# The opening of a fused attention block on one core: loads, casts and squares rearranged, a gate's tanh and a rotary product moved

## The chip, the cores and the metric

The kernel runs on one core of one Trainium2 chip. A core has a tensor engine (PE, which multiplies matrices and also transposes), a vector engine (DVE), a scalar engine (ACT), GpSimd (POOL), and a queue (SP) from which this kernel starts its DMAs. The engines run side by side, each working its own instructions in order, and wait for each other through semaphores. Matrix products land in PSUM, which DVE and ACT read; the other memory on the core is SBUF. The metric is the device time of one execution in microseconds. Three executions of the kernel before took 598.47, 598.74 and 599.65 us; the median, 598.74, is the time to beat.

## The reference

One decoder block for 512 tokens (16 learned meta tokens in front), width 1024, float32: a normalised input, one joint projection, two attention branches (a latent-attention branch with rotary positions, and one with a forget gate), gates, and an output projection.

```
u = rmsnorm(h, pre_norm_g)                      # h: 528 x 1024
proj = u @ w_in                                 # 1024 x 7600
(cq, ckv, k_pe_raw, z_mla, fq, fk, fv, f_logit, z_fox, gate_a, gate_b) = split(proj)
q  = rmsnorm(cq)  @ w_uq ;  kv = rmsnorm(ckv) @ w_ukv
k_pe = rope(k_pe_raw, pos)
o_mla = attention(q, k, v, scale)               # 16 heads, causal
o_fox = attention(fq, fk, fv, scale, cumulative log forget gate)
y_mla = (o_mla * silu(z_mla)) @ w_br_mla ;  y_fox = (o_fox * silu(z_fox)) @ w_br_fox
mixed = (sigmoid(gate_a) * y_mla + sigmoid(gate_b) * y_fox) @ w_out
out = (h + rmsnorm(mixed))[16:]
```

## The kernel before

Tokens are worked in tiles: tiles 0 to 3 hold 128 real tokens each, tile 4 the 16 meta tokens. A float32 product is made of three products of rounded parts: every operand `x` is split into a high part (`xh`, a cast) and a low part (`xl`, the difference), and `mm` is called for high x high, low x high and high x low. That is why each weight is cast (`wsh`, `wh`) and then subtracted (`wsl`, `wl`), and why every transposed activation is written twice, `uTh` by ACT and `uTl` by DVE.

The opening does, for every tile `t`: load it (`load_h`, tile `ht`); sum its squares and take the reciprocal root (`squares`, which leaves the result in `st`); scale it into `hn` (`scaled`); transpose it on PE in two halves of four blocks of 128 columns, each half in one PSUM bank (`turn`, tile `pt`); write `uTh` and `uTl` from the bank, block by block (`turned`; the tile of meta tokens in `turned_all`); and multiply with the small weights, the 432 columns of `w_in` for `cq`, `ckv`, `k_pe_raw` and the forget gate (`small`, result `psm`, accumulated over eight blocks `k`). `back` then normalises and rotates `psm` into `sm`, and `latent` transposes that (`pc`). The small weights come in four loads of two blocks each (`wsr`, two DMAs per load), are cast by `small_hi` and subtracted by `small_lo`. The vector `gcol` holds the gain of the first norm, transposed on PE from `g8` (the product `gps`).

At the start PE multiplies a zero tile (`spun`), and it does so again where it would wait. For PE, the program order is the written order (a manual schedule). On the other engines a scheduler orders the instructions by priority, except for those handed to `pin`, which stay in the order in which they are written. `issue_after` places an instruction behind a given one of its engine.

After the opening, the products of queries, keys, values and gates (`fq`, `fk`, `v`, `z`, `pg`) are interleaved with the attention of eight pairs of heads, two branches each. An attention stage computes scores (`st`), exponentials (`sf`), and in `norm` the normalised weights `pn`, a high part by ACT and a low part by DVE; then a transposing DMA and the product with the values. `z_unit` makes a gate: the product `z`, a tanh on ACT into `sil`, and a product on DVE that reads the accumulator again. Accumulators come from a pool of three PSUM buffers (`acc`), which the next products take in turn as they come free.

Of the kernel before, what the change touches and what calls it, by code (L numbers as in the profile page):

```python
# [22 lines left out]
D = 1024  # L23
# [31 lines left out]
def block_kernel(ctx: ExitStack, tc: tile.TileContext, x, meta_tokens, pre_norm_g, w_in, fox_forget_b,  # L55
# [201 lines left out]
    with ExitStack() as ph:  # L257
# [28 lines left out]
        load_h(1)  # L286
# [10 lines left out]
        def small_hi(c, copy):  # L297
            return copy(wsh[:, 2 * c : 2 * c + 2, :], wsr[c])

        def small_lo(c, eng):  # L300
            cs = slice(2 * c, 2 * c + 2)
            return eng.tensor_tensor(out=wsl[:, cs, :], in0=wsr[c], in1=f32(wsh[:, cs, :]), op=ALU.subtract)
# [19 lines left out]
        def squares(t, pin):  # L322
# [5 lines left out]
            if t == 0:  # L328

                for i, sl in enumerate(halves):  # L330
                    pin(nc.scalar.activation(hn[:, sl], ht[:, sl], AF.Square, accum_out=st1[:, 2 + i : 3 + i]))
                pin(nc.vector.tensor_scalar(out=st1[:, 0:1], in0=st1[:, 2:3], scalar1=1.0 / D, scalar2=EPS, op0=ALU.mult,
                                            op1=ALU.add))
                pin(nc.scalar.activation(st1[:, 1:2], st1[:, 3:4], AF.Sqrt, bias=st1[:, 0:1], scale=1.0 / D))
# [5 lines left out]
        def scaled(t, pin):  # L340
            rows = 128 if t < 4 else META
            for sl in halves if t == 0 else [slice(0, D)]:
# [39 lines left out]
        def small(t, which, ks=range(KD)):  # L382

            d0, q0 = (META + 128 * t, 0) if t < 4 else (0, R_Q)
            if t not in psms:
                psms[t] = acc("psm4")[:, 0:NSM] if t == 4 else pps.tile([128, NSM], F32, tag="psm", name=f"psm{t}")
            ts = slice(d0, d0 + 128)
            for k in ks:
                for q, (u, w) in enumerate(((uTh, wsh), (uTl, wsh), (uTh, wsl))):
                    if q in which:  # L390
                        mm(psms[t][:, q0:], u[:, k, ts], w[:, k, q0:], start=(k == 0 and q == 0),
                           stop=(k == KD - 1 and q == 2))

        def back(t):
# [10 lines left out]
            tm = pa.tile([128, 2, 2, 16], F32, tag="tm", name=f"tm{t}")  # L405
            for i in range(2):
                for cs in range(2):
                    nc.vector.tensor_tensor(out=tm[:rows, i, cs], in0=psm[:rows, k0 + 16 * i : k0 + 16 * i + 16],
                                            in1=rt[:rows, t, 2 * i + cs], op=ALU.mult)
            nc.vector.tensor_tensor(out=sm[:rows, k0 : k0 + 32].rearrange("p (a b) -> p a b", a=2), in0=tm[:rows, 0],  # L410
                                    in1=tm[:rows, 1], op=ALU.add)
            rstd(st2[:rows, 2 + both[0][2] : 4], st2[:rows, both[0][2] : 2], 1, 0, rows)
            nc.scalar.copy(sm[:rows, k0 + 32 :], psm[:rows, k0 + 32 :])
# [32 lines left out]
        scaled(0, pin)  # L446
        pin(nc.vector.tensor_copy(gcol, gps[:, 0, 0:KD]))
        turn(0)
        for _ in range(4):
            mm(spun, KP[1][:, 0:128], KP[1][:, 0:512], start=True, stop=True)  # L450
        squares(1, pin)
        scaled(1, pin)
        for c in range(3):
            pin(small_hi(c, nc.gpsimd.tensor_copy))
        turned(0, 0, range(KD), pin)
        small(0, (0,), range(2))
        turn(1)
        turned(0, 1, range(KD), pin)
        pin(small_lo(0, nc.gpsimd))
        turned(1, 0, range(KD), pin)  # L460
        turned(1, 1, range(KD), pin)
        pin(small_hi(3, nc.scalar.copy))
        small(0, (1,), range(2))
        small(0, (0, 1), range(2, 6))
        small(1, (0, 1), range(6))
        small(0, (0, 1), range(6, KD))
        small(1, (0, 1), range(6, KD))
        for c in (1, 2, 3):
            pin(small_lo(c, nc.vector))
# [6 lines left out]
        small(0, (2,))  # L476
# [58 lines left out]
    with ExitStack() as att:  # L535
# [26 lines left out]
        masks = []  # L562
# [163 lines left out]
        def attention(br, pr):  # L726
# [64 lines left out]
            def norm(g):  # L791
                def fn():
# [14 lines left out]
                    for b in GRP[g]:  # L807
                        for h in range(2):
# [5 lines left out]
                            nc.scalar.activation(hi, sf, AF.Copy, scale=rib)  # L814
# [400 lines left out]
```

## Time and profile before

| what | value |
|---|---|
| median of three executions | 598.74 us |
| the profiled execution | 598.62 us |
| its span on the core | 596.5 us |
| PE busy | 588.3 us (99%) |
| DVE busy | 380.2 us (64%) |
| ACT busy | 343.3 us (58%) |
| POOL busy | 201.6 us (34%) |

The span runs from the first to the last instruction in the profile; the profiled execution's own time is 2.1 us longer. All places in time below are microseconds from the start of the span. A row of the profile in order of time reads: start, duration, engine, source line, operation, the tile written and the tiles read, partitions x elements, count; in brackets stands how long the engine had idled before, and who released it. Several rows of one kind that follow each other are merged, and the duration is then that of the whole group. In the chain of waits each step goes back to what released the one after it.

### The profile page before, as it was taken

Reading aid. Unit: us, or ns where it says so; the run is one execution under the profiler, and the core shown is the slowest. Engines: PE = TensorE matmul, PEld = TensorE weight load, DVE = VectorE, ACT = ScalarE, POOL = GpSimd, SP = SyncE. Lnnn points to the kernel's source line nnn. Section 1 sums busy time; section 2 is a strip of 40 time slices with the busy share of each in tenths; the row PEclk is TensorE's granted clock in tenths of the full one; section 3 lists DMA queues with packets and bytes.
Section 4 is the critical chain, followed back from the end, with each engine's and each line's share of the span. In section 5 each row is a group of like instructions: output and inputs, shape, how many; then the busy total and the mean of one; then the engine's idle time right before and its main releaser. Section 6 shows DMA issues by size and latency. Waiting matters only on the chain.

```text
span 596.5 us, 10744 instructions
## 1 busy us (share of the span) xinstructions
PE 588.3 (99%) x3697; PEld 497.3 (83%) x3697; DVE 380.2 (64%) x1096; ACT 343.3 (58%) x785; POOL 201.6 (34%) x271
## 2 busy tenths in 40 slices
PE   8999999999999999999999999999999999999996
PEld 7989779889888888798898898878888888888884
DVE  5944876775776775757758747855634524367857
ACT  7846775784774775757748747842123423353753
POOL 3317646455458463544544544430000000000000
PEclk9999999999999999999999999999999999999999
DMA  8535599999994998896986987978523332333503
GB/s 295 119 78 170 122 173 248 219 175 232 166 218 113 221 220 219 185 188 166 177 197 166 194 162 154 194 166 297 168 77 100 105 105 73 106 106 102 215 2 141
DMA packets 219998, 97.45 MB, mean 163 GB/s; under 512 B 131456, under 2 KB 209672, under 8 KB 219944
## 3 DMA queue, kind: packets, MB, share of 16 engines
q1 hardware_dynamic: 219944, 96.77, 70.1%
q8 instruction: 29, 0.48, 0.3%
q14 instruction: 25, 0.20, 0.1%
HBM read 62.36 MB, written 3.97 MB: 111 GB/s over the span
## 4 chain that ended last, share of the span: by engine, by line
PE 95%; ACT 1%; DVE 1%; DMA 1%; issue 0%; SPq 0%; POOL 0%; DVEq 0%; ACTq 0%; POOLq 0%
PE z L97 16%; PE pg L97 15%; PE py L97 15%; PE v L97 9%; PE st L97 8%; PE fk L97 8%; PE fq L97 8%; PE ov L97 5%; PE x L97 4%; PE psm L97 3%; PE mq L97 2%; PE mk L97 1%; PE ppe L97 1%; PE y L97 1%; DMA wsr<-in_w_in_dram 1%; ACT uTh L367 0%
## 5 line engine op out<-in xcount | busy, mean ns | idle before, releaser
L103 POOL TENSOR_TENSOR wl<-wraw,wh 128x1024 fp32r<-128x1024 f32 (+2 forms) x62 | 119.5, 1935 | 92.8 <-ACT wh L130 70.0
L130 ACT CAST wh<-wraw 128x1024 fp32r<-128x1024 f32 (+1 forms) x80 | 83.1, 1043 | 116.0 <-PE pg L97 38.5
L787 ACT ACTIVATE sf<-sf,nb 128x272 f32<-128x272 f32 (+3 forms) x128 | 72.5, 568 | 16.5 <-DVE nb L779 15.0
L815 DVE SCALAR_TENSOR_TENSOR pn<-sf,ri,pn 128x128 f16<-128x128 f32 (+3 forms) x128 | 68.6, 576 | 6.7 <-ACT pn L814 6.4
L103 DVE TENSOR_TENSOR wl<-wraw,wh 128x1024 fp32r<-128x1024 f32 x34 | 41.6, 1222 | 42.4 <-ACT wh L130 42.4
L814 ACT ACTIVATE pn<-sf,ri 128x128 f16<-128x128 f32 (+3 forms) x128 | 61.3, 550 | 9.3 <-ACT sf L787 7.4
L97 PE MATMUL z<-uTh,wh 128*128 128x512 f32 x128 | 50.9, 398 | 0.0
L97 PE MATMUL pg<-uTh,wh 128*128 128x512 f32 x128 | 50.3, 393 | 0.0
L97 PE MATMUL z<-uTl,wh 128*128 128x512 f32 x128 | 50.1, 392 | 0.0
L97 PE MATMUL z<-uTh,wl 128*128 128x512 f32 x128 | 50.0, 390 | 0.0
L97 PE MATMUL pg<-uTh,wl 128*128 128x512 f32 x128 | 49.8, 389 | 0.0
L97 PE MATMUL pg<-uTl,wh 128*128 128x512 f32 x128 | 49.8, 389 | 0.0
L97 PE MATMUL py<-gh,wh 128*128 128x512 f32 x128 | 49.8, 389 | 0.0
L97 PE MATMUL py<-gl,wh 128*128 128x512 f32 x128 | 49.8, 389 | 0.0
L97 PE MATMUL py<-gh,wl 128*128 128x512 f32 x128 | 49.8, 389 | 0.0
L97 PE MATMUL st<-hlk,hlq 64*128 64x272 f32 (+3 forms) x480 | 45.5, 308 | 0.0
L97 PEld LDWEIGHTS st<-hlk,hlq 64*128 64x128 f32 x480 | 34.6, 185 | 6.0 <-ACT vh L702 2.8
L683 DVE TENSOR_REDUCE vsc<-v 128x1 f32<-128x272 f32 (+1 forms) x32 | 13.2, 433 | 39.9 <-PE v L97 39.9
L97 PE MATMUL v<-uTh,wl 128*128 128x256 f32 (+1 forms) x128 | 36.5, 285 | 0.0
L97 PE MATMUL fk<-uTl,wh 128*128 128x256 f32 (+1 forms) x128 | 36.4, 285 | 0.0
L97 PE MATMUL fk<-uTh,wh 128*128 128x256 f32 (+1 forms) x128 | 36.4, 285 | 0.0
L97 PE MATMUL v<-uTl,wh 128*128 128x256 f32 (+1 forms) x128 | 36.4, 285 | 0.0
(233 smaller groups left out, 1461.5 us busy)
## 6 DMA issues: line engine op xcount, KB each, us to landing
wraw<-in_w_in_dram SPq DMA_DIRECT2D x56, 512.0 KB, 4.5
cbp<-c_dram SPq DMA_DIRECT2D x16, 264.0 KB, 4.7
wraw<-in_w_br_fox_dram SPq DMA_DIRECT2D x8, 512.0 KB, 8.3
tb<-in_w_out_dram SPq DMA_DIRECT2D x8, 512.0 KB, 4.9
wraw<-in_w_br_mla_dram SPq DMA_DIRECT2D x8, 512.0 KB, 3.4
wraw<-in_w_out_dram SPq DMA_DIRECT2D x6, 512.0 KB, 3.7
xr<-in_x_dram SPq DMA_DIRECT2D x4, 512.0 KB
out_dram<-yo SPq DMA_DIRECT2D x8, 256.0 KB, 2.0
```

The lines of the kernel that those rows point to most:

```text
L97: nc.tensor.matmul(*a, **k)
L103: return eng.tensor_tensor(out=lo, in0=src, in1=f32(hi), op=ALU.subtract)
L130: nc.scalar.copy(wh[:, :n], raw[:, :n])
L683: nc.vector.tensor_reduce(out=sc[:, i : i + 1], in_=ps, op=ALU.max, axis=AX.X, apply_absolute_value=True)
L787: exps[g] = nc.scalar.activation(sf, sf, AF.Exp, bias=sums["nb"][:, h, b : b + 1], scale=-1.0, accum_out=sums["su"][:, h, b : b + 1]).ins
L814: nc.scalar.activation(hi, sf, AF.Copy, scale=rib)
L815: nc.vector.scalar_tensor_tensor(out=lo, in0=sf, scalar=rib, in1=hi, op0=ALU.mult, op1=ALU.subtract)
```

## The change

It has these parts:

- SP: the first load of the small weights is issued ahead of tile 1's load instead of behind it.
- Casts and subtractions of the small weights go by single blocks of 128 rows (432 columns) instead of pairs (864): of the casts, four are now on ACT (blocks 1, 3, 5, 7) and four on POOL; of the subtractions, blocks 0 and 1 go singly and 2-3 together to POOL, 4-5 and 6-7 to DVE.
- The squares of tile 1 are made in halves, one on DVE and one on ACT, as are its scalings; between them stand the first copies of tile 0.
- The spins of PE: five, then `gps`, then three; and three after the first `psm` products of tile 0, of which there are now five ahead of tile 1's transposes instead of two.
- `back`: the second pair of rotary products is written to free columns of the PSUM bank of `psm` instead of SBUF.
- The tanh of the first forget-branch gate (pair 0) is put behind the last of the stage's `pn` copies on ACT.

```diff
-        load_h(1)
...
             wsr.append(r)
+            if c == 0:
+                load_h(1)
+
+        def small_hi(k, copy):
+            return copy(wsh[:, k, :], wsr[k // 2][:, k % 2, :])
...
+        def squares(t, pin, first=lambda: None, second=lambda: None):
...
+            if t < 2:
                 for i, sl in enumerate(halves):
+                    sums = st1[:, 2 + i : 3 + i]
+                    if t and i == 0:
+                        pin(nc.vector.tensor_tensor_reduce(out=hn[:, sl], in0=ht[:, sl], in1=ht[:, sl], scale=1.0, scalar=0.0,
+                                                           op0=ALU.mult, op1=ALU.add, accum_out=sums))
+                    else:
+                        pin(nc.scalar.activation(hn[:, sl], ht[:, sl], AF.Square, accum_out=sums))
+                first()
+                plus, root = (3, 2) if t else (2, 3)
+                pin(nc.vector.tensor_scalar(out=st1[:, 0:1], in0=st1[:, plus : plus + 1], scalar1=1.0 / D, scalar2=EPS, op0=ALU.mult,
                                             op1=ALU.add))
+                second()
+                pin(nc.scalar.activation(st1[:, 1:2], st1[:, root : root + 1], AF.Sqrt, bias=st1[:, 0:1], scale=1.0 / D))
...
-            tm = pa.tile([128, 2, 2, 16], F32, tag="tm", name=f"tm{t}")
+            tm = [pa.tile([128, 2, 16], F32, tag="tm", name=f"tm{t}"), psm[:, NSM : NSM + 32].rearrange("p (c f) -> p c f", c=2)]
...
-        for _ in range(10):
-            mm(spun, KP[1][:, 0:128], KP[1][:, 0:512], start=True, stop=True)
+        spin(5)
         gps = ppt.tile([128, 4, 128], F32, tag="pt", name="gps")
         tps(gps[:, 0, 0:KD], g8, ident[0:KD, 0:KD])
+        spin(3)
         squares(0, pin)
+        scaled(0, pin, lambda: pin(nc.vector.tensor_copy(gcol, gps[:, 0, 0:KD])))
         turn(0)
+        pin(small_hi(0, nc.gpsimd.tensor_copy))
+        pin(small_lo(0, 1, nc.gpsimd))
+        turned(0, 0, range(2), pin)
+        pin(small_hi(1, nc.scalar.copy))
+        turned(0, 1, range(2), pin)
+
+        def before_sum():
+            turned(0, 0, range(2, 4), pin)
+            turned(0, 1, [2], pin)
+        squares(1, pin, before_sum, lambda: turned(0, 1, [3], pin))
         scaled(1, pin)
+        turned(0, 0, range(4, 6), pin)
...
+        small(0, (0,), range(2))
+        small(0, (1,), range(2))
+        small(0, (2,), [0])
+        spin(3)
         turn(1)
...
-                with tc.high_priority(offset=60):
+                with tc.high_priority(offset=60), nullcontext() if pr or not br else tc.issue_after(normed[0]):
                     ins = nc.scalar.activation(sil, pz, AF.Tanh, scale=0.5)
```

How the instructions stand now, at three places. In these rows stand the source line, the operation, the tile written and the tiles read, the size, and a count; tile numbers behind a name tell buffers apart. PE at the start of the program, before (`hn_169` is tile 0 scaled, `hn_193` tile 1):

```order
L97 MATMUL spun<-KPL 128x512 x10
L100 MATMUL gps<-ident,g_119 128x8
L100 MATMUL pt_0_179<-ident,hn_169 128x128 x4
L100 MATMUL pt_1_184<-ident,hn_169 128x128 x4
L97 MATMUL spun<-KPL 128x512 x4
L97 MATMUL psm_210<-wsh,uTh 128x432 x2
L100 MATMUL pt_0_213<-ident,hn_193 128x128 x4
L100 MATMUL pt_1_218<-ident,hn_193 128x128 x4
L97 MATMUL psm_210<-wsh,uTl 128x432 x2
```

The same place in the changed program (`hn_167` is tile 0, `hn_194` tile 1):

```order
L97 MATMUL spun<-KPL 128x512 x5
L100 MATMUL gps<-ident,g_119 128x8
L97 MATMUL spun<-KPL 128x512 x3
L100 MATMUL pt_0_177<-ident,hn_167 128x128 x4
L100 MATMUL pt_1_182<-ident,hn_167 128x128 x4
L97 MATMUL psm_217<-wsh,uTh 128x432 x2
L97 MATMUL psm_217<-wsh,uTl 128x432 x2
L97 MATMUL psm_217<-wsl,uTh 128x432
L97 MATMUL spun<-KPL 128x512 x3
L100 MATMUL pt_0_226<-ident,hn_194 128x128 x4
L100 MATMUL pt_1_231<-ident,hn_194 128x128 x4
```

Three more products of tile 0 now stand ahead of tile 1's transposes, and three spins between. ACT between the root for tile 0 and the first copies of tile 1, before; in brackets are the semaphores that a row waits for, named by the engine or the DMA that raises them:

```order
L334 ACTIVATE st_0_170<-st_0_170 128x1 [waits DVE_49,Activation_49]
L337 ACTIVATE hn_193,st_1_194<-ht_122 128x1024 [waits DMAHW3_49]
L317 ACTIVATE st_1_194<-st_1_194,eps_t 128x1 [waits Activation_49]
L367 ACTIVATE uTh<-pt_0_179,gcol 128x128 [waits DVE_49,PE_49]
L367 ACTIVATE uTh<-pt_0_179,gcol 128x128 x3
```

ACT at the same place in the changed program, down to tile 0's fifth copy:

```order
L343 ACTIVATE st_0_168<-st_0_168 128x1 [waits DVE_49,Activation_49]
L378 ACTIVATE uTh<-pt_0_177,gcol 128x128 [waits DVE_49,PE_49]
L378 ACTIVATE uTh<-pt_0_177,gcol 128x128
L299 CAST wsh<-wsr_124 128x432 [waits DMAHW4_49,DMAHW3_49]
L337 ACTIVATE hn_194,st_1_195<-ht_127 128x512 [waits DMAHW5_49]
L378 ACTIVATE uTh<-pt_0_177,gcol 128x128 [waits DVE_49]
L378 ACTIVATE uTh<-pt_0_177,gcol 128x128
L343 ACTIVATE st_1_195<-st_1_195 128x1 [waits DVE_49]
L378 ACTIVATE uTh<-pt_1_182,gcol 128x128 [waits PE_49]
```

Tile 1's Square and root stood ahead of all copies of tile 0; now two copies and a cast stand ahead of its Square, and two copies between the Square and the root. DVE in that stretch of the changed program (the instruction named ISA is the half of the squares, with the read of its sum):

```order
L375 SCALAR_TENSOR_TENSOR uTl<-pt_0_177,gcol,uTh 128x128 [waits DVE_49,PE_49,Activation_49]
L375 SCALAR_TENSOR_TENSOR uTl<-pt_0_177,gcol,uTh 128x128
L334 ISA hn_194,st_1_195<-ht_127 128x512 [waits DMAHW5_49]
L334 ISA st_1_195 128x1
L375 SCALAR_TENSOR_TENSOR uTl<-pt_0_177,gcol,uTh 128x128 [waits Activation_49]
L340 TENSOR_SCALAR st_1_195<-st_1_195 128x1
L375 SCALAR_TENSOR_TENSOR uTl<-pt_0_177,gcol,uTh 128x128
L344 RECIPROCAL st_1_195<-st_1_195 128x1 [waits Activation_49]
L354 TENSOR_SCALAR hn_194<-ht_127,st_1_195 128x512 [waits DVE_49]
```

The small sum that ACT's root needs (L340) stands behind a `uTl` that waits for ACT's copies. ACT in the first attention stage, before:

```order
L814 ACTIVATE pn_715<-sf_873,ri_872 128x2x128 [waits Activation_49] x2
L718 ACTIVATE sil_1043<-z_957 128x512 [waits PE_49]
L814 ACTIVATE pn_715<-sf_873,ri_872 128x3x128 [waits Activation_49]
L814 ACTIVATE pn_715<-sf_873,ri_872 128x3x128
L814 ACTIVATE pn_716<-sf_921,ri_872 128x4x128 [waits DVE_49,Activation_49]
L814 ACTIVATE pn_716<-sf_921,ri_872 128x4x128 [waits Activation_49]
L244 CAST hlq_1055<-mq_1048 128x512 [waits PE_49]
```

And in the changed program:

```order
L845 ACTIVATE pn_720<-sf_878,ri_877 128x2x128 [waits Activation_49] x2
L845 ACTIVATE pn_720<-sf_878,ri_877 128x3x128 [waits Activation_49]
L845 ACTIVATE pn_720<-sf_878,ri_877 128x3x128
L845 ACTIVATE pn_721<-sf_926,ri_877 128x4x128 [waits DVE_49,Activation_49]
L845 ACTIVATE pn_721<-sf_926,ri_877 128x4x128 [waits Activation_49]
L749 ACTIVATE sil_1048<-z_962 128x512 [waits PE_49]
L244 CAST hlq_1060<-mq_1053 128x512 [waits PE_49]
```

The tanh `sil` went from ahead of four copies to behind them; its product on DVE moved likewise, behind the four low parts of `pn`.

More of the change, by code (lines that the diff above doesn't have):

```diff
@@ L295, in block_kernel, with small_lo @@
             wsr.append(r)
[L297 to L302, printed above, removed]
+            if c == 0:
+                load_h(1)
+        def small_hi(k, copy):
+            return copy(wsh[:, k, :], wsr[k // 2][:, k % 2, :])
+        def small_lo(k, n, eng):
+            c, k0 = k // 2, k % 2
+            return eng.tensor_tensor(out=wsl[:, k : k + n, :], in0=wsr[c][:, k0 : k0 + n], in1=f32(wsh[:, k : k + n, :]), op=ALU.subtract)
         for t in (2, 4, 3):
@@ L385, in small @@
             if t not in psms:
-                psms[t] = acc("psm4")[:, 0:NSM] if t == 4 else pps.tile([128, NSM], F32, tag="psm", name=f"psm{t}")
+                psms[t] = acc("psm4") if t == 4 else pps.tile([128, 512], F32, tag="psm", name=f"psm{t}")
             ts = slice(d0, d0 + 128)
@@ L475, in block_kernel @@
         scaled(3, pin)
-        small(0, (2,))
+        small(0, (2,), range(1, KD))
         sms = {0: back(0)}
```

64 lines of the change are left out of this document (33 added, 31 removed).

## Prediction

> **What bounds the kernel now.** I read the page first (busy time, chain by line), then the chain of waits of the first 60 us, then each engine in order of time around every place that the change touches.
>
> ```profile
> span 596.5 us, 10744 instructions
> PE 588.3 (99%) x3697; PEld 497.3 (83%) x3697; DVE 380.2 (64%) x1096; ACT 343.3 (58%) x785; POOL 201.6 (34%) x271
> PE 95%; ACT 1%; DVE 1%; DMA 1%; issue 0%; SPq 0%; POOL 0%; DVEq 0%; ACTq 0%; POOLq 0%
> ```
>
> The tensor engine (PE) bounds everything: 95% of the chain is PE work. A microsecond can be won or lost only where PE idles, spins on the warming product `spun`, or waits. A delay of PE early on is not absorbed later, because no other engine is close to being the limit. The opening is the first such place.
>
> ```profile
> 2.94 4.83 DMA wsr<-in_w_in_dram
> ...
> 7.89 0.91 POOL wsh L298
> ...
> 10.49 7.63 PE psm L97 x38
> ```
>
> These are start, duration and work. The chain starts with the load of the first quarter of the small weights, which lands at 2.94 + 4.83 = 7.77; POOL casts it, and then PE runs `psm`.
>
> ```profile
> 1.45 4.63 PE L97 MATMUL spun<-KPL 128*128 128x512 f32 x10 [1.45 <-DVE KPL L231]
> ...
> 6.25 1.44 PE L100 MATMUL pt<-ident,hn 128*128 128x128 f32 x8
> 7.44 1.17 PE L97 MATMUL spun<-KPL 128*128 128x512 f32 x4
> 8.85 0.66 PE L97 MATMUL psm<-wsh,uTh 128*128 128x432 f32 x2 [0.24 <-POOL wsh L298]
> 9.40 1.09 PE L100 MATMUL pt<-ident,hn 128*128 128x128 f32 x8
> ...
> 17.96 1.63 PE L100 MATMUL pt<-ident,hn 128*128 128x128 f32 x16
> 10.24:17.96 7.72, 7.71 (x38) 6.98 (x38) 0.00 (x0) 0.00 (x0) 1.00 1.04 332
> ```
>
> PE in order of time, and last the `psm` products alone between 10.24 and 17.96: 38 products in 7.72 us, 0.203 us each, no gap. From 9.40 on PE is full. What precedes is 1.41 us (7.44 to 8.85) of spinning and waiting. So the mark to watch is the start of the third tile's transposes, 17.96 now: both kernels have done the same real work there (all 40 `psm` products that precede it).
>
> **The change, part by part.**
>
> *Loads.* SP issues the first quarter of the small weights ahead of token tile 1. Nothing else on SP changes place.
>
> ```profile
> 3.46 0.63 ACT L331 ACTIVATE hn<-ht 128x512 f32<-128x512 f32 x1 [1.24 <-DMA ht<-in_x_dram]
> 3.99 0.19 ACT L331 ACTIVATION_READ_ACCUMULATOR hn<-ht 128x1 f32 x1
> ...
> 5.18 0.29 ACT L334 ACTIVATE st<-st 128x1 f32<-128x1 f32 x1
> 6.38 1.06 ACT L337 ACTIVATE hn<-ht 128x1024 f32<-128x1024 f32 x1 [0.90 <-DMA ht<-in_x_dram]
> ...
> 7.76 2.15 ACT L367 ACTIVATE uTh<-pt,gcol 128x128 fp32r<-128x128 f32 x8
> 10.09 2.17 ACT L367 ACTIVATE uTh<-pt,gcol 128x128 fp32r<-128x128 f32 x8 [0.18 <-PE pt L100]
> ...
> 12.10 0.97 ACT L298 CAST wsh<-wsr 128x864 fp32r<-128x864 f32 x1
> ```
>
> Tile 1 lands just before 6.38 now and the quarter at 7.77. The bytes of the two together are the same, so after the swap tile 1 lands at about 7.8, 1.4 us later, and the quarter about 1.4 us earlier, at 6.4. The statistics of tile 1, which PE needs for its next transposes, thus start later; the products that need only the quarter start earlier.
>
> *Tile 1's chain to PE.* In the new order of ACT and DVE, tile 1's squares stand behind two `uTh` copies and a cast, and the sum behind two more `uTh` copies and a `uTl` of tile 0. In the built program ACT and DVE take turns on one transposed bank: `uTl` waits for the copies ahead of it, the next copies wait for `uTl`.
>
> ```profile
> 5.50 0.16 DVE L335 RECIPROCAL st<-st 128x1 f32<-128x1 f32 x1 [1.14 <-ACT st L334]
> 5.70 0.88 DVE L343 TENSOR_SCALAR hn<-ht,st 128x512 f32<-128x512 f32 x2
> ...
> 8.09 1.26 DVE L343 TENSOR_SCALAR hn<-ht,st 128x1024 f32<-128x1024 f32 x1
> 9.27 4.21 DVE L364 SCALAR_TENSOR_TENSOR uTl<-pt,gcol,uTh 128x128 fp32r<-128x128 f32 x16
> ...
> 16.49 0.75 DVE L343 TENSOR_SCALAR hn<-ht,st 128x1024 f32<-128x1024 f32 x1
> 7.89 0.90 POOL L298 CAST wsh<-wsr 128x864 fp32r<-128x864 f32 x1 [6.11 <-DMA wsr<-in_w_in_dram]
> 9.31 0.91 POOL L298 CAST wsh<-wsr 128x864 fp32r<-128x864 f32 x1 [0.52 <-DMA wsr<-in_w_in_dram]
> ...
> 11.47 2.06 POOL L302 TENSOR_TENSOR wsl<-wsr,wsh 128x864 fp32r<-128x864 f32 x1
> ```
>
> The first half of tile 0 is transposed by about 7.2 (8 transposes from 6.25 to 7.44). From there: two copies at 0.25 (8 take 2.15, the last ending 0.4 after its step), 7.7; cast of 432 columns, half of 0.97, 8.2; Square of half a tile 0.53 + 0.19, 8.9; two copies, the second out at 9.55; `uTl` 0.26 (16 in 4.21), 9.85; the small sum on DVE 0.15, 10.0; root 0.29, 10.35; reciprocal 0.16, 10.55; scaling of half a tile 0.44, 11.0. POOL's `wsl` of 432 columns (half of 2.06, behind a cast that starts at 9.31 as now) runs from about 9.8 to 10.8, and scaling beside POOL's cast took 1.26 instead of 0.75 at 8.09. That adds 0 to 0.5; I take 0.2. Transposes of tile 1 start at 11.2 instead of 9.40. The half of the squares on DVE has no row; between 0.44 (scaling of as many columns) and 1.06 (a whole tile on ACT) it ends by 9.4, ahead of the copies it runs beside, and costs nothing.
>
> *What PE does meanwhile.* Five `psm` products instead of two, then three spins, which end near 10: PE idles about 1.2 us. After the transposes (0.85, as from 9.40 to 10.25) five products are ready, to 13.1. The next one needs `uTl` of tile 1, and that waits for four `uTh` copies of tile 1, between which ACT makes a cast: ACT is through tile 0 at 11.6, first half of tile 1 transposed at 11.75, four copies and the cast 1.5, out at 13.35; `uTl` 0.33; PE resumes at 13.75, another 0.6 us idle. The remaining 30 products take 30 x 0.203 = 6.1: the third tile's transposes start at 19.85, against 17.96. **Opening: +1.9 us.** Bounds: +1.3 (no POOL wait and the second idle stretch halved), +2.7 (POOL's wait in full, tile 1 landing half a microsecond later). I keep the sum because each step has its own row. ACT's extra casts (four of 432 for one of 864, +0.97) less half a Square are hidden behind PE's 6 us stretch; DVE must have tile 2 scaled by 19.85 and gets there near 18.9 (its `uTl` out at 16.0, two `wsl` of about 1.0, scaling 0.75).
>
> *Rotary product.* One factor of the pair now lies in PSUM.
>
> ```profile
> 23.99 5.99 POOL L103 TENSOR_TENSOR wl<-wraw,wh 128x1024 fp32r<-128x1024 f32 x3 [10.46 <-ACT wh L130]
> 24.55 1.88 DVE L410 TENSOR_TENSOR sm<-tm 128x32 f32<-128x32 f32 x1
> ...
> 27.47 0.27 DVE L103 TENSOR_TENSOR KPL<-pc,KPH 32x128 fp32r<-32x128 f32 x1
> 27.40 0.35 PE L97 MATMUL psm<-wsl,uTh 128*128 128x432 f32 x1
> 27.88 0.63 PE L100 MATMUL pc<-ident,sm 128*128 128x128 f32 x4
> ```
>
> A sum of 32 columns took 1.88 us beside POOL's work; DVE's `KPL`, queued behind it, ends at 27.74, and PE's `pc`, 0.48 after the product before it instead of 0.20, starts right after. With the stall gone PE gains 0.28. **-0.3 us** (0 to -0.4).
>
> *Gate's tanh.* In the first attention stage it now stands behind the last four `pn` copies.
>
> ```profile
> 74.15 0.29 PE L97 MATMUL mk<-cTh,wl 128*128 128x272 f32 x1
> 74.98 0.39 PE L97 MATMUL mk<-cTh,wh 128*128 128x256 f32 x1 [0.54 <-DVE hlq L103]
> 70.62 0.60 ACT L718 ACTIVATE sil<-z 128x512 f32<-128x512 f32 x1 [1.28 <-PE z L97]
> 71.11 2.34 ACT L814 ACTIVATE pn<-sf,ri 128x384 f16<-128x384 f32 x4
> 71.25 0.69 DVE L719 SCALAR_TENSOR_TENSOR sil<-sil,z 128x512 f32<-128x512 f32 x1 [1.39 <-ACT sil L718]
> 71.85 2.47 DVE L815 SCALAR_TENSOR_TENSOR pn<-sf,ri,pn 128x384 f16<-128x384 f32 x4
> 74.24 0.68 DVE L103 TENSOR_TENSOR hlq<-mq,hlq 128x512 fp32r<-128x512 f32 x1
> ```
>
> ACT idles 1.28 us for the gate's product with four copies ready behind the tanh, and DVE likewise; so `hlq` frees its accumulator at 74.92, and PE starts the second `mk` 0.83 after the first's last product, where 0.12 would do. Moved: copies from 69.34, tanh near 71.7, DVE's `pn` done near 72.4, gate's product 73.05, `hlq` 73.7, before PE asks at 74.27. **-0.7 us.** What is late next is the gate's own accumulator, free at 73.05 and needed at 73.89: 0.8 us of room.
>
> Sum: 1.9 - 0.3 - 0.7 = +0.9. The profiled execution took 598.62, 0.12 under the median of 598.74, so the sum lands at 599.5 on it and 599.6 on the median: +0.15%, inside the 0.2% (1.2 us) that a measurement of this kernel can tell from no change.
>
> [...] Ten spins took 4.63 us, 0.46 each, and four later ones 1.17, 0.29 each: PE begins slow and is faster by 7.4, after staying busy since 1.45. The new order stops spinning earlier and leaves two idle stretches before 13.75. [...] The sum above, with PE waiting and not computing until 13.75, would change little unless the slow rate lasted beyond that.
>
> **Rivals.**
> 1. *The clock stays slow past 13.75.* Before, PE was fast about 5.5 us after it began to be busy; counted from 11.2, that is 16.7. Three microseconds of products at half speed cost 1.5 us more: 601.1; half of that if counted from the five products at about 8: 600.3. Against it: spins and transposes fill most of the time until 7.4 also in the new order.
> 2. *The tanh's gain is not had.* If ACT and DVE run 0.8 us later there than reckoned, PE waits on the gate's accumulator at the first `mk` instead: 600.3. For it: the room is narrow; against it: all rows ahead of it are unchanged.
> 3. *A cheap opening.* POOL and DVE miss each other, tile 1's copies come sooner: +1.3 or less, 598.9.
> 4. *Faster.* The opening breaks even if tile 1's transposes start by about 9.9 and the second idle stretch does not appear; landing at 7.8 plus Square 0.72, root 0.29, reciprocal 0.16, scaling 0.44 gives 9.45 at best. Then three products (0.6) are ahead, and the opening is worth -0.55: 597.2. The order on ACT speaks against it: four copies and a cast stand in that chain.
>
> **How the numbers follow.** Forecast 599.6 (its own range 599.0 to 600.4): 0.50, of which 0.36 within 1.2 us of 598.74 and 0.14 above, where the opening costs 2.3 or more. Rival 1: 0.17 (0.03 within, 0.14 above). Rival 2: 0.15 (0.03 and 0.12). Rival 3: 0.12, all within. Rival 4: 0.06 (0.04 faster, 0.02 within). Together faster 0.04, same 0.56, slower 0.40. The range 598.5 to 601.0 leaves out most of rival 4 and the far end of rival 1.
>
> **What would show it.** Right: tile 1's transposes near 11.2, with `hn` as releaser; a wait of PE on `uTl` near 13.7; third tile at 19.5 to 20.2; DVE's sum of 32 columns at 0.2 us; no gap between the two `mk` halves. Wrong: transposes of tile 1 before 10.2, products of 432 columns still 0.36 apart after 14, or a new PE wait at the first `mk`.

## The result and the profile after

The changed kernel takes 600.48 us (median of 9, 599.77 to 601.82) against 598.74 before (now a median of nine as well): a ratio of 1.0026, 95% interval 1.0018 to 1.0035. Measured once more beside other kernels it gave 600.06 (median of 12) and 1.0018 (1.0009 to 1.0026). So it is slower, by 0.2 to 0.3%. The ratios and their intervals, here and below, are not quotients of the medians and can differ from them a little. One execution of the kernel with tanh and rotary factor but without the opening took 646.38 us at a granted clock of 0.85 and is left out of its ratio. The profiled execution of the changed kernel took 600.92, with a span of 599.1; the one before took 598.62, with 596.5.

First the page of the changed kernel: span, PE's busy time, and the chain by engine.

```profile
span 599.1 us, 10748 instructions
PE 589.0 (98%) x3694; PEld 497.8 (83%) x3694; DVE 380.4 (63%) x1099; ACT 344.1 (57%) x788; POOL 204.0 (34%) x274
...
PE 91%; issue 3%; DMA 2%; ACT 2%; DVE 1%; POOL 1%; SPq 0%; DVEq 0%; POOLq 0%; ACTq 0%
```

PE's busy time has hardly moved (588.3 to 589.0) while the span grew by 2.6, so most of the time went into waits. PE's share of the chain fell from 95% to 91%. That is no measure of lost time, as 4% of the span would be 24 us: the chain now leaves PE for a stretch and goes by way of late loads, which the views below show.

PE of the changed kernel in order of time (start, duration, work, and what ended the idle time before it):

```profile
1.45 2.50 PE L97 MATMUL spun<-KPL 128*128 128x512 f32 x5 [1.45 <-DVE KPL L231]
4.91 0.24 PE L100 MATMUL gps<-ident,g 8*128 8x8 f32 x1 [0.96 <-DMA g<-in_pre_norm_g_dram]
5.08 1.65 PE L97 MATMUL spun<-KPL 128*128 128x512 f32 x3
6.53 1.91 PE L100 MATMUL pt<-ident,hn 128*128 128x128 f32 x8
8.13 1.33 PE L97 MATMUL psm<-wsh,uTh 128*128 128x432 f32 x2
9.26 0.93 PE L97 MATMUL psm<-wsh,uTl 128*128 128x432 f32 x2
...
10.34 1.00 PE L97 MATMUL spun<-KPL 128*128 128x512 f32 x3
11.38 1.34 PE L100 MATMUL pt<-ident,hn 128*128 128x128 f32 x8
...
13.36 0.35 PE L97 MATMUL psm<-wsh,uTh 128*128 128x432 f32 x1
14.11 0.47 PE L97 MATMUL psm<-wsh,uTl 128*128 128x432 f32 x1 [0.40 <-DVE uTl L375]
...
20.12 1.04 PE L100 MATMUL pt<-ident,hn 128*128 128x128 f32 x8
```

The mark, the third tile's transposes, stands at 20.12 against 17.96: the opening costs 2.16 us in this pair of traces. Tile 1's transposes start at 11.38 (9.40 before), and PE waits for `uTl` until 14.11. What the prediction had not pictured is the pace: PE now waits 0.96 us for the gains, in the middle of its spins; tile 0's eight transposes take 1.6 us (6.53 to 8.13) where they took 1.2, and the two `uTl` products and the one after them are 0.36 apart until 10.34, against 0.20 later. The granted clock is on record, as full, from 10.64 on (from 7.01 before). Up to there PE runs at about half its later rate: the spins of 512 columns are 0.427 us apart, the last of them 0.233 (0.427 and 0.231 before).

What fed tile 1's transposes, on the scalar and the vector engine of the changed kernel:

```profile
7.62 0.63 ACT L378 ACTIVATE uTh<-pt,gcol 128x128 fp32r<-128x128 f32 x2 [1.99 <-PE pt L100]
8.14 0.55 ACT L299 CAST wsh<-wsr 128x432 fp32r<-128x432 f32 x1
8.58 0.64 ACT L337 ACTIVATE hn<-ht 128x512 f32<-128x512 f32 x1
...
9.20 0.63 ACT L378 ACTIVATE uTh<-pt,gcol 128x128 fp32r<-128x128 f32 x2
10.31 0.29 ACT L343 ACTIVATE st<-st 128x1 f32<-128x1 f32 x1 [0.48 <-DVE st L340]
...
10.13 0.14 DVE L340 TENSOR_SCALAR st<-st 128x1 f32<-128x1 f32 x1
...
10.84 1.17 DVE L354 TENSOR_SCALAR hn<-ht,st 128x512 f32<-128x512 f32 x2
```

Tile 1's Square starts at 8.58, its small sum at 10.13, the root at 10.31 and the scaling at 10.84. Now the two places that gain, in the same kernel: the rotary sum and `pc`, then the `pn` copies, the tanh, `hlq` and `mk`.

```profile
26.83 0.19 DVE L421 TENSOR_TENSOR sm<-tm,psm 128x32 f32<-128x32 f32 x1
29.70 0.60 PE L100 MATMUL pc<-ident,sm 128*128 128x128 f32 x4
70.65 2.74 ACT L845 ACTIVATE pn<-sf,ri 128x256 f16<-128x256 f32 x5
73.29 0.57 ACT L749 ACTIVATE sil<-z 128x512 f32<-128x512 f32 x1
74.75 0.68 DVE L103 TENSOR_TENSOR hlq<-mq,hlq 128x512 fp32r<-128x512 f32 x1
75.95 0.29 PE L97 MATMUL mk<-cTh,wl 128*128 128x272 f32 x1
76.08 0.28 PE L97 MATMUL mk<-cTh,wh 128*128 128x256 f32 x1
```

The rotary sum takes 0.19 instead of 1.88, and `mk`'s second half follows the first by 0.13. Matching PE's work of the two kernels piece by piece gives the whole account of how far the changed kernel is behind: 2.16 us at the third tile, 2.10 at the last product ahead of `pc`, 1.81 from `pc` on (-0.29), 1.10 from the second half of `mk` on (-0.71). Then comes what the prediction had no term for: 2.12 from the second half of `v` on, near 99 us (+1.02), 2.45 at the next `ov` (+0.33), 2.26 a little later (-0.19), and 2.27 at the end.

The place at `v`, in the chain of waits of the changed kernel, then on its scalar engine, vector engine and PE:

```profile
80.25 6.11 DMA wraw<-in_w_in_dram
...
86.38 1.05 ACT L130 CAST wh<-wraw 128x1024 fp32r<-128x1024 f32 x1 [0.52 <-DMA wraw<-in_w_in_dram]
...
90.97 1.05 ACT L130 CAST wh<-wraw 128x1024 fp32r<-128x1024 f32 x1 [1.13 <-DMA wraw<-in_w_in_dram]
...
98.29 0.68 DVE L103 TENSOR_TENSOR hlq<-fq,hlq 128x512 fp32r<-128x512 f32 x1
...
99.03 0.38 PE L97 MATMUL v<-uTh,wh 128*128 128x256 f32 x1 [0.96 <-DVE hlq L103]
```

and the same casts and `hlq` in the kernel before:

```profile
84.77 1.03 ACT L130 CAST wh<-wraw 128x1024 fp32r<-128x1024 f32 x1
88.12 1.03 ACT L130 CAST wh<-wraw 128x1024 fp32r<-128x1024 f32 x1
...
95.48 0.69 DVE L103 TENSOR_TENSOR hlq<-fq,hlq 128x512 fp32r<-128x512 f32 x1
```

Before, neither cast (of `wraw`, weights for the next stage's queries and keys) waited for its data. Now both do, and behind them on the scalar engine stand the `pn` copies and the exponentials, behind those the vector engine's `pn` and `hlq`, and behind `hlq` PE's accumulator for `v`. PE loses about 1.0 us at this place; `hlq` starts 2.8 us later than before.

### The profile page after: what moved, and what is told of

Read it like the earlier page. It is cut to its first block, busy times and chain, and to the rows that moved or that the text cites. A ratio compares the mean times of both kernels' runs of the same rounds, so it can differ in the third digit from the quotient of the medians.

```text
span 599.1 us, 10748 instructions
## 1 busy us (share of the span) xinstructions
PE 589.0 (98%) x3694; PEld 497.8 (83%) x3694; DVE 380.4 (63%) x1099; ACT 344.1 (57%) x788; POOL 204.0 (34%) x274
## 4 chain that ended last, share of the span: by engine, by line
PE 91%; issue 3%; DMA 2%; ACT 2%; DVE 1%; POOL 1%; SPq 0%; DVEq 0%; POOLq 0%; ACTq 0%
PE z L97 15%; PE pg L97 15%; PE py L97 15%; PE v L97 8%; PE st L97 8%; PE fk L97 7%; PE fq L97 7%; PE ov L97 5%; PE x L97 4%; PE psm L97 3%; PE mq L97 2%; PE mk L97 1%; DMA wraw<-in_w_in_dram 1%; PE ppe L97 1%; PE y L97 1%
## 5 line engine op out<-in xcount | busy, mean ns | idle before, releaser
L818 ACT ACTIVATE sf<-sf,nb 128x272 f32<-128x272 f32 (+3 forms) x128 | 72.5, 568 | 15.7 <-DVE nb L810 14.2
L97 PE MATMUL v<-uTh,wh 128*128 128x256 f32 (+1 forms) x128 | 36.5, 285 | 1.0 <-DVE hlq L103 1.0
```

Source lines behind the costliest of these rows:

```text
L97: nc.tensor.matmul(*a, **k)
L818: exps[g] = nc.scalar.activation(sf, sf, AF.Exp, bias=sums["nb"][:, h, b : b + 1], scale=-1.0, accum_out=sums["su"][:, h, b : b + 1]).ins
```

## The experiments

Each ran beside the kernel before on the same chip; ratios are to it.

**The tanh alone**, in the kernel before.

```
...
-                with tc.high_priority(offset=60):
+                with tc.high_priority(offset=60), nullcontext() if pr or not br else tc.issue_after(normed[0]):
                     ins = nc.scalar.activation(sil, pz, AF.Tanh, scale=0.5)
...
-                            nc.scalar.activation(hi, sf, AF.Copy, scale=rib)
+                            normed[:] = [nc.scalar.activation(hi, sf, AF.Copy, scale=rib).ins]
```

> The kernel before with the gate's tanh alone moved behind the last four `pn` copies. Theory A (the gain at `mk` is kept; the wait of 1.0 us on `hlq` at the second half of `v`, near 99 us in the changed kernel, has another cause): PE is 0.7 us ahead from the second `mk` on and stays so, 598.0. Theory B (PE takes the 0.7 at `mk`, the weights on SP's queue do not follow, and the scalar engine's casts and the exponentials behind them come late): PE waits about 1.0 us at the second half of `v` and the time is 599.0.

It took 598.44, a ratio of 0.9998 (0.9989 to 1.0007): no change that can be told. In the trace PE is 0.65 us ahead of before from the second `mk` on, and 0.20 of it is lost at `v`: here too the second of the two weight loads was late.

```profile
84.02 1.03 ACT L130 CAST wh<-wraw 128x1024 fp32r<-128x1024 f32 x1
...
89.51 1.05 ACT L130 CAST wh<-wraw 128x1024 fp32r<-128x1024 f32 x1 [2.06 <-DMA wraw<-in_w_in_dram]
```

So in this trace B does not hold (no full microsecond comes back), nor does A in full: the gain is made at `mk`, and a part of it was lost 20 us later. The times, 597.68 to 600.23, spread over 2.5 us, those of the kernel before over 1.4.

**The rotary factor alone**, in the kernel before.

```
...
-            tm = pa.tile([128, 2, 2, 16], F32, tag="tm", name=f"tm{t}")
+            tm = [pa.tile([128, 2, 16], F32, tag="tm", name=f"tm{t}"), psm[:, NSM : NSM + 32].rearrange("p (c f) -> p c f", c=2)]
...
```

> The kernel before with one factor of the rotary pair in PSUM, nothing else. Theories A and B alike: DVE's sum of 32 columns takes 0.2 us instead of 1.88, the gap of 0.48 ahead of the first `pc` shrinks to 0.2, PE is 0.3 us ahead to the end: 598.45. If the gain is lost later: 598.7.

It took 598.56, 0.24 us less in the medians, a ratio of 0.9997 (0.9988 to 1.0006). The sum takes 0.19, and PE gains 0.28 at `pc` and keeps it. The size is as expected; the times alone could not tell it from nothing.

**The opening alone**: the changed kernel with the tanh's and the rotary lines put back.

```
...
-            tm = [pa.tile([128, 2, 16], F32, tag="tm", name=f"tm{t}"), psm[:, NSM : NSM + 32].rearrange("p (c f) -> p c f", c=2)]
+            tm = pa.tile([128, 2, 2, 16], F32, tag="tm", name=f"tm{t}")
...
-                with tc.high_priority(offset=60), nullcontext() if pr or not br else tc.issue_after(normed[0]):
+                with tc.high_priority(offset=60):
...
```

> The changed kernel without the moved tanh and without the rotary factor in PSUM: the new opening alone. Theory A and B: third tile's transposes at 20.1 (2.2 us later than before), no wait at the second half of `v`, 600.9. Rival C (the wait at `v` comes from the opening, by the place at which a code fetch meets the weight loads): the wait of about 1.0 us at `v` is there too, 601.9.

It took 600.68, a ratio of 1.0031 (1.0020 to 1.0043): +1.88 us in the medians. The third tile's transposes start at 20.26, there is no wait at `v`, and the old gap at `mk` is back. In this trace the opening by itself does not make the wait at `v`, which speaks against C.

**Tanh and rotary factor without the opening**: the first two edits together, in the kernel before.

> The kernel before with the moved tanh and the rotary factor, without the new opening. Theory A: -0.7 and -0.3 add, 597.75, faster than both kernels. Theory B: the gain at `mk` is lost at `v`, 598.7.

It took 597.86, a ratio of 0.9984 (0.9975 to 0.9993): 0.94 us faster than the kernel before and 2.2 to 2.6 below the changed one. The loads were in time, and PE did not wait at `v`. So this beats both kernels, and with the opening alone the two parts add up to +1.88 - 0.94 = +0.94. The changed kernel lost +1.74 and +1.21 in its two measurements. The rest, 0.3 to 0.8, would belong to the parts being together, but the interval of each of these ratios reaches half a microsecond or more to either side, so it is not shown that there is a rest at all.

**The changed kernel again**, with no edit.

> The changed kernel once more, nothing altered. Theory L (the wait at the second half of `v` comes from late loads: of the sixteen shares of the two weight loads issued near 80.5 us one landed 2 and 5 us behind the other fifteen, when a code fetch of 16 KB at 83.5 fell between them): it varies from execution to execution, so the median lies between 599.7 (opening +2.2, rotary -0.3, tanh -0.7, no late share) and 601, and in this profile the wait at `v` is there if and only if a share of the loads is over 1 us behind the others. Theory B (it is in the order of the program): the same wait of about 1.0 us, whatever the loads do; 600.5.

It took 600.06. In this trace the second cast waits 1.79 us for its load, and PE loses 0.19 at `v`, not 1.02: the loads come late again, and how much reaches PE differs. Where PE lost time at `v` (1.02, 0.19 and 0.20 in the changed kernel, this one and the tanh alone) a cast had waited for a load; in none of the other traces did either happen. The view of DMA issues gives the median time from issue to landing of the two loads, here before and in the changed kernel:

```profile
wraw<-in_w_in_dram SPq DMA_DIRECT2D x2, 512.0 KB, 4.7
wraw<-in_w_in_dram SPq DMA_DIRECT2D x2, 512.0 KB, 8.1
```

It is 4.4 with tanh and rotary factor, 7.9 in this trace and 7.0 with the tanh alone. Each of these loads has sixteen landing events in the trace, which I take for one for each share of its bytes. In the changed kernel fifteen of the sixteen shares of each load land in time (by 84.34 and 85.80) and one comes late (86.36 and 90.94); in this trace it is the same (85.41 and 90.74), and with the tanh alone only the second load has a late share (89.49).

**The loads moved ahead on SP's queue**, in the changed kernel.

```
                 low[0] = nc.gpsimd
+                for load in [fn.load for _, fn in fills[1] if hasattr(fn, "load")][:3]:
+                    load()
                 n1()
```

> The changed kernel with the two weight loads of the second stage's queries and keys issued ahead of the first stage's four `pt` transposes on SP's queue instead of behind them (near 71 instead of 80.5). Theory L: the casts find their data, no wait at `v`, third tile's transposes still at 20.1, 599.7 in most executions and a smaller spread; at worst the transposes come 1.2 us later and PE waits up to 0.5 for them at `ov`. Theory B: the wait at `v` stays, 600.5.

It took 605.65, a ratio of 1.0117 (1.0100 to 1.0134): both theories were wrong about this edit.

```profile
87.20 3.11 PE L97 MATMUL ov<-pt,vp 80*64 80x512 f16 x18 [4.11 <-DMA pt<-pn]
```

The loads were issued at 70.9, and the four `pt` transposes behind them took SP from 72.0 to 84.6 instead of 71.0 to 80.2; PE waited 4.1 us for the last. The wait at `v` is gone because everything else is later, so it tells the two theories nothing. It shows what a place in that queue was worth here: 1 MB put ahead of four transposes cost 4.1 us of waiting, and 1.6 more as PE, after it, ran its first products at half rate (the granted clock was 0.5 from 87.44 to 90.85).

**Code fetches moved.** The page counts 29 fetches of 16 KB on the instruction queue ("q8 instruction: 29, 0.48, 0.4%"), one to some 127 of PE's 3694 products; from one fetch to the next PE starts 70 to 168 products in the changed kernel's trace and 90 to 162 before. In the changed kernel one starts at 83.53, while both loads are under way. Forty tiny products ahead of the third tile bring the later fetches forward against the work around them.

```
+        for _ in range(40):
+            mm(spun[:, 0:16], KP[1][:, 0:128], KP[1][:, 0:16], start=True, stop=True)
         turn(2)
```

> The changed kernel with forty products of 16 columns ahead of the third tile's transposes: they cost about 2.5 us there, which shifts every engine and every queue alike, and they bring each later code fetch of the tensor engine (16 KB, one for some 128 products with their weight loads) about 5 us earlier against the work around it. Theory L: the fetch near 83.5 now comes ahead of the two weight loads, all sixteen shares of each land within 0.5 us, no wait at the second half of `v`; PE is as far behind before at the end as at the second `mk`. Theory B: shares and fetches do not matter, PE waits 0.2 to 1.0 us at `v` as in the changed kernel.

It took 607.70; what the forty products cost, beyond 2.5, is told at the end. The fetch fell at 86.45, 3.0 us ahead of the first load (89.48), the loads took 4.5 from issue to landing, all shares within 0.5, and PE did not wait at `v`; it waited 0.8 for the transposes at `ov`. That is as L expects. But a fetch within a load does not always make a share late: it began while the second load was under way with the tanh alone (83.20), but also with the rotary factor alone (83.26), in the kernel before (83.62) and with tanh and rotary factor (83.76), and only the first of these had a late share. So the wait at `v` goes with a late share in every trace; that the fetch makes the share late is not shown, and these traces speak against the fetch as the whole cause.

**Spins in one piece**, in the changed kernel.

```
-        spin(5)
+        spin(10)
         gps = ppt.tile([128, 4, 128], F32, tag="pt", name="gps")
         tps(gps[:, 0, 0:KD], g8, ident[0:KD, 0:KD])
-        spin(3)
```

> The changed kernel with the old ten spins in one piece ahead of the transpose of the gains, in place of five, the transpose and three. Theory T3 (the opening's excess over the forecast is the clock, full only from 10.6 us, because the wait of 1 us for the gains broke the busy stretch): the clock is full from 7.0, the eight transposes of tile 0 end near 7.4 instead of 8.1, tile 1's start near 11.0 instead of 11.4, the third tile's at 19.7 instead of 20.1: 0.4 us faster than the changed kernel. Theory T2 alone (the orders on the scalar and vector engine set the opening): third tile's transposes stay within 0.15 of 20.1.

It took 600.61 (598.66 to 601.69), a ratio of 1.0023 (1.0012 to 1.0035): no different from the changed kernel. In the trace the first half went as T3 expects: full rate from 6.6, five products done by 9.1. Then tile 1, one share of which landed at 9.02 (the other fifteen by 7.60), kept PE idle for 2.43 us, and the clock fell again (low from 13.44 to 16.86):

```profile
9.12 0.85 PE L97 MATMUL spun<-KPL 128*128 128x512 f32 x3
12.40 1.50 PE L100 MATMUL pt<-ident,hn 128*128 128x128 f32 x8 [2.43 <-DVE hn L354]
...
14.06 0.56 PE L97 MATMUL psm<-wsh,uTl 128*128 128x432 f32 x1
14.43 0.56 PE L97 MATMUL psm<-wsh,uTh 128*128 128x432 f32 x1
```

Products are 0.36 apart from 14.06 to 16.6, and the third tile's transposes start at 22.03. An early fast clock did not help here, as PE then had to wait for tile 1.

**The old order of loads in the new opening**, in the changed kernel.

```
         gcol = pa1.tile([128, KD], F32, tag="gcol", name="gcol")
+        load_h(1)
...
-            if c == 0:
-                load_h(1)
```

> The changed kernel with the old order of loads: tile 1 ahead of the first quarter of the small weights. Theory T1 (tile 1's later landing, 7.8 instead of 6.4, sets the opening): tile 1's transposes at about 10.0 and the third tile's 1.4 us earlier, at 18.7. Theory T2 (its statistics stand behind two copies and a cast on the scalar engine, which end at 8.6 in any case): tile 1's transposes between 11.2 and 11.9, as five products now wait for POOL's cast of a quarter that lands at 7.8; third tile's at 20.0 to 20.6.

It took 600.88, a ratio of 1.0033 (1.0021 to 1.0045): not better than the changed kernel, so T1, which wanted 1.4 us less, falls for this opening. In the trace the loads themselves were late (tile 1 at 7.34, the quarter at 8.71, against 6.35 and 7.77 before), tile 1's transposes started at 12.82, the clock stayed slow until 15.7, and the third tile's transposes stood at 21.99, all worse than T2 had it.

**The new order of loads alone**, in the kernel before.

```
-        load_h(1)
...
             wsr.append(r)
+            if c == 0:
+                load_h(1)
```

> The kernel before with the two loads in the new order and nothing else changed. Theory T1: the landing of tile 1 near 7.8 carries the whole loss, third tile's transposes near 20, 600.8. Theory T2: it carries about half: squares of the whole tile from 7.85, root at 9.3, scaling at 9.7, tile 1's transposes at 10.3 to 10.5 instead of 9.40, third tile's at 18.8 to 19.1, 599.8; the rest of the loss is the order on the scalar and vector engine.

It took 600.39, a ratio of 1.0028 (1.0017 to 1.0040): between the two theories, with times in two groups, eight from 599.12 to 600.68 and four from 601.64 to 602.50. The profiled execution is of the second:

```profile
9.69 0.63 PE L97 MATMUL psm<-wsh,uTh 128*128 128x432 f32 x2 [1.67 <-ACT uTh L368]
10.96 1.43 PE L100 MATMUL pt<-ident,hn 128*128 128x128 f32 x8 [0.64 <-DVE hn L344]
12.04 1.07 PE L97 MATMUL psm<-wsh,uTl 128*128 128x432 f32 x2
12.91 0.56 PE L97 MATMUL psm<-wsh,uTh 128*128 128x432 f32 x1
...
14.35 0.56 PE L97 MATMUL psm<-wsh,uTh 128*128 128x432 f32 x1
14.71 0.49 PE L97 MATMUL psm<-wsh,uTl 128*128 128x432 f32 x1
15.04 0.36 PE L97 MATMUL psm<-wsh,uTh 128*128 128x432 f32 x1
```

Tile 1's squares, ahead of tile 0's copies in that order, hold the scalar engine until it lands (7.79), PE idles 1.67 and 0.64 us, and the clock is low from 11.57 to 14.98. By the ratios, the new order of loads alone costs about as much as the whole new opening (1.0031), though there the scalar engine's wait for tile 1 makes the delay and not the work between squares and scaling.

**Tile 1's statistics in one piece**, in the changed kernel.

```
-        squares(1, pin, before_sum, lambda: turned(0, 1, [3], pin))
+        squares(1, pin)
         scaled(1, pin)
+        before_sum()
+        turned(0, 1, [3], pin)
...
-        spin(3)
         turn(1)
```

> The changed kernel with tile 1's sum, root, reciprocal and scaling right behind its squares, ahead of the `uTh` copies and `uTl` that stood between them, and without the three spins ahead of its transposes. Theory T2 (the work put between tile 1's squares and its scaling sets the opening): the sum starts at 9.4 instead of 10.13, tile 1's transposes between 10.5 and 10.9 instead of 11.38, the third tile's 0.4 to 0.7 us earlier than in the changed kernel, 19.4 to 19.7, if loads and clock are as there. Theory T1 (the landing of tile 1 near 7.8 sets it, what stands between is hidden): transposes at 11.2 or later, third tile's within 0.2 of 20.1.

```profile
10.28 0.66 PE L100 MATMUL pt<-ident,hn 128*128 128x128 f32 x4 [0.34 <-DVE hn L354]
11.52 0.66 PE L100 MATMUL pt<-ident,hn 128*128 128x128 f32 x4 [0.58 <-DVE hn L354]
```

Tile 1's transposes start at 10.28, 2.55 after its landing (7.73) where the changed kernel needs 3.55; the third tile's start at 19.35. The trace sides with T2. But the profiled execution was the fastest of eleven (598.81), and the median, 600.04 with a ratio of 1.0013 (1.0004 to 1.0021), is not clearly below the changed kernel's.

**The same in the opening alone** (the edit above and that of the opening alone together), to have it free of what happens at `v`.

> The new opening alone (without the moved tanh and the rotary factor) with tile 1's sum, root, reciprocal and scaling right behind its squares and without the three spins ahead of its transposes. The opening alone stood at a ratio of 1.0031. Theory T2: tile 1's transposes between 10.2 and 10.9, the third tile's at 19.3 to 19.7 instead of 20.26, and 0.6 to 0.9 us less time, a ratio of 1.0017 to 1.0022, nearly 600.0. Against it (what the traces show at the third tile is lost again later, or the clock falls because PE now idles ahead of the transposes): 1.0027 or more.

It took 601.53, a ratio of 1.0040 (1.0026 to 1.0054): not faster than the opening alone, and against T2. Tile 1 landed at 9.00 in this trace; its transposes came 2.23 later (11.23; 3.39 in the opening alone, which had it at 8.11), the third tile's at 20.30. So the chain from landing to transposes is a microsecond shorter, and the time does not show it. Landing and chain add up, and both can be long; whether the idle stretch of 1.22 us ahead of these transposes also costs the clock in some executions, no trace here shows.

## Why the prediction was right and where it fell short

The measured 600.48 lies in the range of 598.5 to 601.0, just above the forecast's own range of 599.0 to 600.4; 600.06 lies in both. The parts can be told one by one.

*Landings.* Tile 1 landed at 7.83 and the quarter at 6.34, as forecast (7.8, 6.4). That they vary from execution to execution had not been reckoned with: with the new order of loads in the new opening tile 1 landed between 7.57 and 9.02 in eight traces.

*Tile 1's chain.* Its transposes start at 11.38 for 11.2, with `hn` as the releaser in the second trace and in the opening alone. Every step came in the forecast order. In the profiled execution the chain started 0.3 to 0.4 late, because tile 0's first transposes ran at half rate (0.213 apart, against 0.109 for tile 1's; first copy at 7.62), and the two scalings beside POOL took 1.17, 0.29 over their 0.88.

*PE meanwhile.* PE was to be done with five products and three spins near 10 and to idle for 1.2 us. In the profiled execution the same work, most of it at half rate (products of 432 columns 0.36 apart), filled the time until 11.3. In the other four traces of this opening the clock was full earlier (from 5.89 to 10.26) and PE idled 0.6 to 1.5 us there, while tile 1's transposes still started between 11.06 and 11.50. The earliest clock was that of the kernel with the code fetches moved:

```profile
8.74 0.86 PE L97 MATMUL spun<-KPL 128*128 128x512 f32 x3
11.06 1.34 PE L100 MATMUL pt<-ident,hn 128*128 128x128 f32 x8 [1.46 <-DVE hn L354]
```

Its forty products begin, where the third tile's transposes would, at 19.82. So the late clock of the changed kernel's trace explains some 0.3 us of its 20.12 and not the opening's cost. The prediction had argued this: a slow rate changes little while PE would wait anyway. The second wait, on `uTl`, was there in all five traces: until 14.11 for 13.75 in the changed kernel.

*Opening, +1.9.* The third tile stood 2.16, 1.92 and 2.30 behind the trace of before in the changed kernel, its repetition and the opening alone, and the latter's median was +1.88. The trace of before was an early one: with the old opening the third tile stands at 17.96, 18.00, 18.22 and 18.52 in four traces, with the new one unchanged at 19.88, 20.12, 20.13 and 20.26, and the two means are 1.9 apart. So the size of this term is shown. How it divides up is not. The work between squares and scaling is worth about a microsecond of tile 1's chain in two traces, as the prediction had it, but taking it out shortened the time in neither kernel clearly, and the new order of loads alone costs about as much as the whole.

*Rotary, -0.3, and tanh, -0.7.* PE gained 0.29 and 0.71. The gate's accumulator, said to be late next, never was: PE did not wait at the first `mk`.

*What the sum had no term for* is a weight load of which one share lands late, one stage behind the moved tanh. The tanh's 0.7 was reckoned to run on to the end of the program, and with the loads in time it did: with tanh and rotary factor PE is 0.56 us behind before at the third tile and 0.49 ahead at the end. The casts had room for it. Before, the two loads landed 2.0 and 3.8 us ahead of their casts (at 82.79 for 84.77 and at 84.28 for 88.12), with tanh and rotary factor still 1.4 and 3.3. A share that is some 5 us late leaves no room in either order: the second load's late shares (89.49 with the tanh alone, 90.94 and 90.74 in the changed kernel) lie behind the places of that cast with the tanh unmoved, 88.12 before and 90.03 in the opening alone.

So the moved tanh takes 0.7 us from the room of the casts; that it makes a share late is not shown. Of the seven traces with the moved tanh, the loads in their place and no added products, three had a share late enough to hold up a cast, and PE lost 0.19 to 1.02 at `v`; a fourth (spins in one piece) had one 1.3 us late, at 88.98, ahead of its cast at 91.03. In the five without the moved tanh no share was over 0.4 us behind the others. These are few traces, and what makes a share late stays open. The missing term could be the 0.3 to 0.8 us by which the changed kernel missed +0.9, as far as the times can tell such a rest.

*The clock.* With the new spins the clock was full from 5.89, 8.93, 9.07, 10.26 and 10.64 us in five traces, with the old ten spins from 4.74 to 7.52 in another five: mostly later. So in four of the five PE was slow for longer, which rival 1 had reckoned with; what brings the full rate, no trace shows. Rival 1, a clock slow past 13.75, did not come in the changed kernel's two traces; it came in three of the other kernels (until 15.0, 15.7 and 16.9, with the third tile at 20.96 to 22.03), in two of them because the clock fell a second time, a way that the rival had not named.

## What to carry to other kernels

A microsecond won on the bounding engine makes the next stage's loads needed a microsecond sooner: ask how long ahead of its first use each of them lands, and what it is issued behind. Here the room was 2.0 and 3.8 us and the gain was kept, except where one share of a load came late. Such a share is felt where the order of an engine has put a cast of it ahead of work that has nothing to do with it. And an opening that trades a steady early start for a better order has to be priced over several traces: identical openings put the third tile up to 0.56 us apart, and the landing of tile 1 alone varied by 1.45 us.

## What was not expected of the hardware

*Forty tiny products did not keep the clock up.* The forty products of 16 columns ran 0.111 us apart without a gap, and within them the clock fell, at about 23.0, and stayed low for 10.2 us:

```profile
19.82 5.67 PE L97 MATMUL spun<-KPL 128*128 128x16 f32 x40
25.33 0.47 PE L100 MATMUL pt<-ident,hn 128*128 128x128 f32 x1
```

Thirty steps at 0.111 and the last ones at 0.213 make 5.5 us for an expected 2.5, and the third tile's products behind them ran 0.36 apart. Being busy was thus not enough in this trace. Whether it matters how much is streamed was not shown; a step of 0.111 held 16 columns there, while a product of 432 takes 0.20.

*It fell with PE idle for no more than 1.67 and 2.43 us at a stretch.* With the loads swapped the clock was full from 4.74 to 11.57 and low until 14.98, that is for 3.41 us. In as long a time ahead of the fall (8.16 to 11.57) PE had run products and transposes for 1.2 us, and its longest pause was 1.67. With the spins in one piece it was low from 13.44 to 16.86, and in the 3.41 us ahead of that fall (10.03 to 13.44) PE had run for 1.0, after its pause of 2.43 to 12.40. In both traces PE had thus been at work for about a third of that time; what makes the clock fall was not shown.

*The start of the full rate wanders.* With the ten spins of the old opening untouched the clock was full from 4.74, 4.75, 6.19, 7.01 and 7.52 us in five traces.

*One share in sixteen.* In four traces a load of 512 KB had fifteen of its sixteen shares landed and the last 1.3 to 5.5 us behind, while in three of them the median from issue to landing (8.1, 7.9 and 7.0, against 4.7 before) looks like that of a slow load.
